# Two encoder layers on one core: the MLP products by one level of Strassen's recursion, with the squared rows kept in DRAM

## The chip, the cores and the metric

The kernel runs on 1 core of one Trainium2 chip. The metric is the device time of one execution in microseconds. Matmuls run on TensorE (PE, with its weight loads as PEld), the other arithmetic on VectorE (DVE), ScalarE (ACT) and GpSimd (POOL); SyncE (SP) issues nearly all DMAs.

## The reference, cut to what matters

Two layers, each with a mixing part (a gated DeltaNet in both directions, a windowed attention, and the sum of both through W_out) and an MLP. x is 1024 rows of 1024 features, D_FF is 4096, everything is float32. The change concerns the last lines of a layer:

```python
mix = (jax.nn.sigmoid(g_ma) * y_a + jax.nn.sigmoid(g_mb) * y_b) @ w_out[l]
x = x + rmsnorm(mix, norm_mix_post[l])

h = rmsnorm(x, norm_mlp_pre[l])                  # 1024 x 1024
u = jnp.square(jax.nn.relu(h @ w_mlp_in[l]))     # 1024 x 4096
x = x + rmsnorm(u @ w_mlp_out[l], norm_mlp_post[l])
```

## The kernel before, in words

A float32 product is made of three fp32r matmuls. Each operand is cut into a high half (a cast on ACT, L149, L165 or L236) and a low half (source minus high half, a subtract on DVE, L150 or L166, or on POOL, L237). `mm3` (L171 to L174) adds high·high, high·low and low·high into one PSUM bank. The moving operand is 128x512, and so is a bank.

A layer goes through stages P1 to P3 (projections, convolution, the two attentions), P4 (output projection, L1060 to L1087) and P5 (MLP, from L1089).

P4 walks the 1024 rows as eight tiles t of 128 rows, four at a time (`hf`), and the output in two column halves `ch`. Per bank there are 24 matmuls (`ps_wo`); DVE copies the bank to `mo` (L1082), ACT squares it for the norm (L1084). After the second half `finish_rows` (L1189) forms the post-norm, adds x, stores the rows to DRAM (`X1d`), forms the MLP's pre-norm, and has `norm_to_T` (L183) transpose the rows on PE (8 transposes of 128x128, L194) and split them into halves: h transposed, `h2T`, in SBUF.

P5 loads W1 and W2 as units of 512 KB (`weight_unit`, L157), splits them, and runs groups of two 128-feature slices: `mlp_in` (L1096) makes u transposed for two slices (per slice and half of the rows 24 matmuls into `ps_m`), with relu and square on ACT (L1113, L1114) and the low half on DVE (L1115, L1116); u stays in SBUF as halves. `mlp_out` (L1119) takes the slices of a group as the contraction and makes for every t and `ch` a partial bank, which DVE adds to an accumulator `acc` in SBUF (L1137). The last group has four slices; there each row tile is finished as soon as its two banks are in (`mlp_finish`, L1148): the norm, the sum with the rows from `X1d`, the store, and in layer 0 the next layer's pre-norm and transposes (`hTn`). The next layer's first matmuls are those of `ps_zA` (128x336, 192 of them), which read `hTn` tile by tile.

The order on an engine is set by a scheduler that works from the code, priorities and buffers; `InOrder` (L140 on) pins an engine's instructions to the order in which they are written. Buffers are pools with a number of copies each: a new tile in a full pool waits for the oldest to be read.

Of the kernel before, what the change touches and what calls it, by code (L numbers as in the profile page):

```python
# [16 lines left out]
P = 128  # L17
# [29 lines left out]
def shape_constants():  # L47
# [28 lines left out]
def trunk(ctx, tc, x, w_in, conv_w, a_log, dt_bias, dn_norm_w, attn_sink, w_up_a, w_up_b, w_out,  # L76
# [12 lines left out]
    # three blocks of 32 KB a partition, handed on from stage to stage  # L89
# [41 lines left out]
    class InOrder:  # L131
        """An engine; what is issued through it stays in the order in which it is written."""
# [24 lines left out]
    def weight_unit(wp, src, kk, n, name):  # L157
# [3 lines left out]
        pw, bw = (wmain, 3) if i % 5 < 3 else (wp, 2)  # L161
# [9 lines left out]
    def mm3(o, lh, ll, rh, rl, first, last, eng=T):  # L171
        eng.matmul(o, lhsT=lh, rhs=rh, start=first, stop=False)  # L172
        eng.matmul(o, lhsT=lh, rhs=rl, start=False, stop=False)  # L173
        eng.matmul(o, lhsT=ll, rhs=rh, start=False, stop=last)  # L174
# [8 lines left out]
    def norm_to_T(pl, xt, wrow, halves, t, tag, tagb, bank=None):  # L183
# [1050 lines left out]
```

## Time and profile before

| what | value |
|---|---|
| median of 3 runs | 3323.45 us (3322.81 to 3325.22) |
| span of the profiled execution | 3319.1 us, 4.3 us under the median |
| PE busy | 3189.2 us, 96% |
| DVE, ACT, POOL busy | 1878.1, 1101.2, 740.4 us |
| first and last `ps_m` matmul, layer 0 | 967.9 to 1672.0 us |
| first and last `ps_m` matmul, layer 1 | 2609.6 to 3310.0 us |
| `ps_m` matmuls | 6144, one third at each line of `mm3` |

The profile is of one execution. A matmul's duration in it (0.39 us) is from its issue to its end; matmuls overlap, so what one costs in a stream is the distance between starts. DVE, ACT and POOL instructions run one after the other on their engine. Waiting time of an engine that nobody waits for costs nothing.

### The profile page before, as it was taken

To read this page: it belongs to the slowest core of one execution; us is meant where nothing else is said; L and a number is where in the kernel's file an instruction comes from. 1 tells how busy PE (TensorE), PEld (TensorE's weight loads), DVE (VectorE), ACT (ScalarE), POOL (GpSimd) and SP (SyncE) were. 2 spreads that over 40 slices of the span, in tenths; PEclk is the share of its full clock that TensorE was granted. 3 is DMA by queue.
4 is the path that set the end of the run, shared out by engine and by line. 5 is a ranking of instruction groups with operands and counts; after the bars stand their busy time and mean duration, and the time that the engine had idled before them with its cause. 6 is when DMAs were issued, how large, how long until landed. Compare 5 with 4: busy or idle time off the path is not lost.

```text
span 3319.1 us, 47199 instructions
## 1 busy us (share of the span) xinstructions
PE 3189.2 (96%) x18576; PEld 2673.1 (81%) x18576; DVE 1878.1 (57%) x3086; ACT 1101.2 (33%) x1976; POOL 740.4 (22%) x712
## 2 busy tenths in 40 slices
PE   8999999997999999999999999998889999999998
PEld 7878767876888888888898887777778888888887
DVE  4687548735573444444556884585356634444445
ACT  3556433322343212211335664333223421112212
POOL 1354454244210000000023544523442000000000
PEclk9999999899999999999999999998989999999999
DMA  3222498596651111111232226966965411111112
GB/s 131 66 65 72 120 274 218 151 237 186 207 171 51 51 51 51 45 51 40 87 110 60 78 67 176 286 173 180 241 184 188 134 45 46 50 51 51 51 51 102
DMA packets 497142, 385.93 MB, mean 116 GB/s; under 512 B 83716, under 2 KB 446980, under 8 KB 496920
## 3 DMA queue, kind: packets, MB, share of 16 engines
q1 hardware_dynamic: 496920, 382.90, 39.8%
q8 instruction: 147, 2.41, 0.3%
q14 instruction: 75, 0.61, 0.1%
HBM read 277.71 MB, written 105.12 MB: 115 GB/s over the span
## 4 chain that ended last, share of the span: by engine, by line
PE 74%; DVE 9%; DMA 6%; POOL 4%; issue 3%; ACT 2%; SPq 2%; POOLq 0%; ACTq 0%; DVEq 0%
PE ps_m L172 14%; PE ps_m L174 14%; PE ps_m L173 14%; PE ps_scO L139 2%; PE ps_wo L173 2%; PE ps_wo L174 2%; PE ps_wo L172 2%; PE ps_gt L172 2%; PE ps_cv L172 2%; PE ps_gt L174 2%; PE ps_cv L173 2%; PE ps_ub L139 2%; PE ps_cv L174 2%; DMA g<-GR 1%; PE ps_gt L173 1%
## 5 line engine op out<-in xcount | busy, mean ns | idle before, releaser
L1137 DVE TENSOR_TENSOR acc<-ps_m,acc 128x512 f32<-128x512 f32 x448 | 306.8, 690 | 459.1 <-PE ps_m L174 458.1
L172 PE MATMUL ps_m<-h2T,w_w 128*128 128x512 f32 x1024 | 399.1, 390 | 1.9 <-DVE h2T L150 1.9
L172 PE MATMUL ps_m<-w_w,u 128*128 128x512 f32 x1024 | 399.1, 390 | 0.0
L173 PE MATMUL ps_m<-h2T,w_w 128*128 128x512 f32 x1024 | 398.9, 390 | 0.0
L173 PE MATMUL ps_m<-w_w,u 128*128 128x512 f32 x1024 | 398.8, 389 | 0.0
L174 PE MATMUL ps_m<-w_w,u 128*128 128x512 f32 x1024 | 398.7, 389 | 0.0
L174 PE MATMUL ps_m<-h2T,w_w 128*128 128x512 f32 x1024 | 398.7, 389 | 0.0
L1113 ACT ACTIVATE ru<-ps_m 128x512 f32<-128x512 f32 x128 | 76.2, 600 | 866.0 <-PE ps_m L174 866.0
L180 POOL TENSOR_TENSOR frs<-fms,mhalf 128x1 f32<-128x1 f32 x16 | 9.7, 606 | 1361.5 <-DVE fms L178 1345.0
L172 PEld LDWEIGHTS ps_m<-h2T,w_w 128*128 128x128 f32 x1024 | 192.3, 188 | 42.1 <-DVE h2T L150 2.4
L174 PEld LDWEIGHTS ps_m<-h2T,w_w 128*128 128x128 f32 x1024 | 192.3, 188 | 39.8
L174 PEld LDWEIGHTS ps_m<-w_w,u 128*128 128x128 f32 x1024 | 192.3, 188 | 39.8
L172 PEld LDWEIGHTS ps_m<-w_w,u 128*128 128x128 f32 x1024 | 192.4, 188 | 39.7
L173 PEld LDWEIGHTS ps_m<-w_w,u 128*128 128x128 f32 x1024 | 192.3, 188 | 39.6
L173 PEld LDWEIGHTS ps_m<-h2T,w_w 128*128 128x128 f32 x1024 | 192.3, 188 | 39.6
L1115 DVE TENSOR_TENSOR ru<-ru 128x512 f32<-128x512 f32 x128 | 88.3, 692 | 236.8 <-ACT ru L1113 236.8
L166 DVE TENSOR_TENSOR w_w<-st_w,w_w 128x1024 fp32r<-128x1024 f32 x128 | 153.7, 1219 | 5.5 <-ACT w_w L165 5.5
L652 DVE TENSOR_TENSOR ct<-ps_kk,g 128x512 f32<-128x512 f32 x128 | 81.7, 683 | 113.3 <-ACT g L636 68.1
L165 ACT CAST w_w<-st_w 128x1024 fp32r<-128x1024 f32 x128 | 130.9, 1043 | 5.7 <-DMA st_w<-in_w_mlp_in_dram 3.9
L468 DVE SCALAR_TENSOR_TENSOR cv<-pad,cw,cv 128x1024 f32<-128x1024 f32 x96 | 131.0, 1365 | 2.5 <-ACT cv L466 1.3
L675 DVE TENSOR_TENSOR tmpx<-ct 128x30 f32<-128x30 f32 (+14 forms) x240 | 114.5, 477 | 30.1 <-ACT ct L670 22.6
L139 PE MATMUL ps_ub<-obT,w_ub 128*128 128x512 f32 x384 | 120.0, 444 | 0.6 <-DVE tb L139 0.6
(343 smaller groups left out, 7041.4 us busy)
## 6 DMA issues: line engine op xcount, KB each, us to landing
LK<-ct SPq DMA_DIRECT2D x64, 512.0 KB, 6.0
st_w<-in_w_mlp_in_dram SPq DMA_DIRECT2D x64, 512.0 KB, 4.3
st_w<-in_w_mlp_out_dram SPq DMA_DIRECT2D x64, 512.0 KB, 3.4
st_g<-in_w_in_dram SPq DMA_DIRECT2D x32, 512.0 KB, 5.3
TG<-tg SPq DMA_DIRECT2D x64, 256.0 KB, 4.5
g<-GR SPq DMA_DIRECT2D x64, 256.0 KB, 6.3
st_wo<-in_w_out_dram SPq DMA_DIRECT2D x32, 512.0 KB, 4.5
TM<-tm SPq DMA_DIRECT2D x16, 512.0 KB, 3.4
```

What stands on the lines that cost most here:

```text
L139: ins = getattr(self.eng, op)(*a, **k)
L165: A.copy(w[:, 0, :kk * n], st[:, :kk * n])
L166: V.tensor_tensor(w[:, 1, :kk * n], st[:, :kk * n], w[:, 0, :kk * n], ALU.subtract)
L172: eng.matmul(o, lhsT=lh, rhs=rh, start=first, stop=False)
L173: eng.matmul(o, lhsT=lh, rhs=rl, start=False, stop=False)
L174: eng.matmul(o, lhsT=ll, rhs=rh, start=False, stop=last)
L468: V.scalar_tensor_tensor(cv, pad[:, j:j + S], wv[:, j:j + 1], cv, ALU.mult, ALU.add)
L652: V.tensor_tensor(las[d][:, :, h], ps.rearrange("p (t a i) -> p t a i", t=2, a=2), ev.unsqueeze(2).to_broadcast([P, 2, 2, P]), ALU.mult)
L675: V.tensor_tensor(tv, Lx[:, k, k + 1:32].unsqueeze(2).to_broadcast([P, n, m]), Xi[:, k, 0:m].unsqueeze(1).to_broadcast([P, n, m]), ALU.mult)
L1113: A.activation(ru[:, 0], ps, AF.Relu)
L1115: V.tensor_tensor(ru[:, 1], ru[:, 0], ru[:, 0], ALU.mult)
L1137: V.tensor_tensor(acc[:, t, cs], ps, acc[:, t, cs], ALU.add)
```

## The change

One level of Strassen's recursion in Winograd's form cuts both operands of a product into 2x2 blocks and makes seven products of blocks in place of eight, with sums of blocks ahead of them and sums of products behind.

P4. ACT copies the bank to `mo` and squares it from there, POOL adds x to the rows (except for the last tile), and `to_forms` takes the place of `norm_to_T`: row tiles 0 to 3 are split as before (`F1`), and tiles 4 to 7 are combined with them into the block sums of h, three of which are first kept in float32 (`raw23`, `raw4`) and split in P5.

W1. A unit is 256 of the 4096 features (16 units, 7 products of 12 matmuls each). The block sums of W1 are made on POOL (`forms_rest`), split, and multiplied in a written order (`To`, an `InOrder` of PE). Products that are added to an earlier one go into the same bank without a new start, and a copy of the bank is taken between (`X`, `uo`). The first two products of the first four units, which need only tiles 0 to 3 of the rows, are issued ahead (`EARLY`). u, squared on DVE, is stored to DRAM (`Ud`), in float32.

W2. The contraction is cut into four groups of 1024 features. Per group four blocks A of u and four blocks B of W2, 1 MB each, are loaded into slots that a table (`PLACES`) names; block sums are made on POOL in halves of 128x1024 (`sums`); each product takes its two operands through `halves` (two casts on ACT and two subtracts on DVE per operand), 48 matmuls into four banks, and DVE adds the banks to that product's accumulator (in group 0 ACT copies them). In the last group POOL adds the accumulators to one another, and `mlp_finish` runs for tiles 0 to 3 at the last product's start and for tiles 4 to 7 behind its banks.

Matmuls per layer of the MLP: 1344 + 1344 after, 1536 + 1536 before.

```diff
+PLACES = (
...
+            def to_forms(t, xn):
+                c0 = (t % 4) * P
+                cs = slice(c0, c0 + P)
+                pvs = []
+                for q in range(2):
+                    ps = ps_ax("ps_nT", "ab"[q])
+                    for k in range(4):
+                        T.transpose(ps[:, k * P:(k + 1) * P], xn[:, (4 * q + k) * P:(4 * q + k + 1) * P], ident)
+                    pvs.append(ps.rearrange("p (k n) -> p k n", n=P))
+                    if t < 4:
+                        split(F1[:, q, 0, :, cs], F1[:, q, 1, :, cs], pvs[q])
+                if t < 4:
+                    return
+                p12, p22 = pvs
+                t1 = p4.tile([P, 4, P], F32, tag="t1", bufs=2, name="t1")
+                t2, t3, t4 = raw23[:, 0, :, cs], raw23[:, 1, :, cs], raw4[:, 0, :, cs]
+                V.tensor_tensor(t1, p12, F1[:, 0, 0, :, cs], ALU.subtract)
+                G.tensor_tensor(t1, t1, F1[:, 0, 1, :, cs], ALU.subtract)
+                V.tensor_tensor(t2, p22, t1, ALU.subtract)
+                A.copy(F2[:, 1, 0, :, cs], t1)
+                G.tensor_tensor(t4, F1[:, 1, 0, :, cs], t2, ALU.subtract)
+                A.copy(t3, p12)
+                V.tensor_tensor(t3, p22, t3, ALU.subtract)
+                G.tensor_tensor(t4, t4, F1[:, 1, 1, :, cs], ALU.add)
+                V.tensor_tensor(F2[:, 1, 1, :, cs], t1, F2[:, 1, 0, :, cs], ALU.subtract)
+                split(F2[:, 0, 0, :, cs], F2[:, 0, 1, :, cs], p22)
...
-                            V.tensor_copy(mo, ps)
-                            jk = p4.tile([P, 512], F32, tag="jk", bufs=2, name="jk")
-                            A.activation(jk, ps, AF.Square, accum_out=sss[tq][:, ch:ch + 1])
+                            A.copy(mo, ps)
+                            A.activation(ps_ax("ps_jk", "c"), mo, AF.Square, accum_out=sss[tq][:, ch:ch + 1])
...
+                def halves(src, n):
+                    w = whl()
+                    hi, lo = (w[:, h, 0:n].rearrange("p (k n) -> p k n", n=src.shape[-1]) for h in range(2))
+                    split(hi, lo, src)
+                    return hi, lo
...
+                    e, s = wsum(), wsum()
+                    G.tensor_tensor(e[:, 0], a21, a22, ALU.add)
+                    G.tensor_tensor(e[:, 1], a11, a21, ALU.subtract)
+                    G.tensor_tensor(s[:, 0], e[:, 0], a11, ALU.subtract)
+                    G.tensor_tensor(s[:, 1], a12, s[:, 0], ALU.subtract)
+                    s13 = halves(e.rearrange("p a k n -> p (a k) n"), 1024)
+                    s24 = halves(s.rearrange("p a k n -> p (a k) n"), 1024)
+                    return s13, s24, halves(a22, 512)
...
+                def product(bank, w, o, b, first):
+                    for k in range(4):
+                        mm3(bank, w[0][:, o + k, :], w[1][:, o + k, :], b[0][:, k, :], b[1][:, k, :],
+                            first and k == 0, k == 3, To, not first)
...
+                early = []
+                def early_second():
+                    wa, a, uo = early[-1]
+                    product(a, wa, 4, b21, False)
+                    A.copy(uo[:, lo5], a)
+                for u in range(EARLY):
+                    wa, a, uo = forms_first(u), ps_mm("ps_a"), u_tile()
+                    product(a, wa, 0, b11, True)
+                    A.copy(uo[:, hi5], a)
+                    if early:
+                        early_second()
+                    early.append((wa, a, uo))
+                early_second()
...
+                    product(c, s13, 0, t1, True)
+                    if was_early:
+                        unit_tail()
+                        A.copy(X[0], uo[:, hi5])
+                    A.copy(X[3], c)
+                    product(a, s24, 0, t2, was_early)
+                    chain(X[1])
+                    product(c, s24, 4, b22, False)
+                    V.tensor_tensor(uo[:, hi5], X[1], c, ALU.add)
+                    squared(uo, uo)
+                    SY.dma_start(Ud[2 * u], uo)
+                    product(a, s13, 4, t3, False)
+                    chain(X[2])
+                    ut = u_tile()
+                    G.tensor_tensor(ut[:, hi5], X[2], X[3], ALU.add)
...
+                def mlp_finish(t):
...
+                    A.activation(flat(jk), a, AF.Square, accum_out=ss)
                     r = rstd_of(p5, ss, 1, 1.0 / D, "f")
-                    V.scalar_tensor_tensor(a, a, r[:, 0:1], wpost2, ALU.mult, ALU.mult)
-                    V.tensor_tensor(xt, xt, a, ALU.add)
+                    V.scalar_tensor_tensor(a, a, r[:, 0:1], flat(wrows["post"]), ALU.mult, ALU.mult)
+                    (G if i == 0 else V).tensor_tensor(flat(xt), flat(xt), a, ALU.add)
...
+                def granules(q, b):
+                    def cut(v, h):
+                        hi, lo = halves(v[:, 2 * h:2 * h + 2], 1024)
+                        return hi, lo
+                    for h in range(2):
+                        yield cut(q, h), cut(b, h)
...
+                n_prod = 0
+                for g in range(NGR):
+                    at = {n: slot[s] for s, n in PLACES[g].items()}
+                    gs = slice(4 * g, 4 * g + 4)
...
+                    def sums(dst, x, y, op):
+                        for h in range(2):
+                            hs = slice(2 * h, 2 * h + 2)
+                            G.tensor_tensor(at[dst][:, hs], at[x][:, hs], at[y][:, hs], op)
+
+                    for m in ("M1", "M2", "M5", "M6", "M3", "M7", "M4"):
+                        if m == "M1":
+                            pair = "A11", "B11"
+                        elif m == "M2":
+                            pair = "A12", "B21"
+                        elif m == "M5":
+                            sums("E", "A21", "A22", ALU.add)
+                            sums("B11", "B12", "B11", ALU.subtract)
+                            pair = "E", "B11"
+                        elif m == "M6":
+                            sums("A21", "A11", "A21", ALU.subtract)
+                            sums("E", "E", "A11", ALU.subtract)
+                            sums("B12", "B22", "B12", ALU.subtract)
+                            sums("B11", "B22", "B11", ALU.subtract)
+                            pair = "E", "B11"
+                        elif m == "M3":
+                            sums("E", "A12", "E", ALU.subtract)
+                            pair = "E", "B22"
+                        elif m == "M7":
+                            pair = "A21", "B12"
+                        else:
+                            sums("B21", "B21", "B11", ALU.subtract)
+                            pair = "A22", "B21"
...
+                            banks = [bank(tq) for tq in range(4)]
+                            order = [(h, k, tq) for h in range(2) for k in range(2) for tq in range(4)]
+                        have = []
+                        for h, k, tq in order:
+                            if h >= len(have):
+                                have.append(next(grs) if not isinstance(grs, list) else grs[h])
+                            if tq >= len(banks):
+                                banks.append(ps_mm("ps_m2", "m"))
+                            uf, wf = have[h]
+                            ts_ = slice(tq * P, tq * P + P)
+                            mm3(banks[tq], uf[0][:, k, ts_], uf[1][:, k, ts_], wf[0][:, k], wf[1][:, k],
+                                (h, k) == (0, 0), (h, k) == (1, 1), To)
+                            if (h, k) != (1, 1):
+                                continue
+                            dst = acc(m, tq)
+                            if final:
+                                for o in {"M2": ("M1",), "M6": ("M1",), "M3": ("M6", "M5"), "M7": ("M6",),
+                                          "M4": ("M7",)}.get(m, ()):
+                                    G.tensor_tensor(dst, dst, acc(o, tq), ALU.add)
+                            if g == 0:
+                                A.copy(dst, banks[tq])
+                            else:
+                                V.tensor_tensor(dst, banks[tq], dst, ALU.add)
+                            if final and m == "M7":
+                                G.tensor_tensor(acc("M5", tq), acc("M5", tq), dst, ALU.add)
+                            if final and m == "M4":
+                                mlp_finish(4 + tq)
...
```

Three places where the order on an engine moves. First, PE between the output projection (`ps_wo`) and the MLP of layer 0. Before, the transposes of a tile (`ps_nT`) stood among the MLP's first matmuls:

```order
L173 MATMUL ps_m_8935<-h2T_8031,w_w_2_8865 128x512
L174 MATMUL ps_m_8935<-h2T_8031,w_w_2_8865 128x512
L194 MATMUL ps_nT<-ident,xn 128x128 x8
L172 MATMUL ps_m_8935<-h2T_8031,w_w_2_8865 128x512
L173 MATMUL ps_m_8935<-h2T_8031,w_w_2_8865 128x512
```

Now 24 early matmuls stand ahead of all transposes of tiles 4 to 7, and the other 72 early ones behind them:

```order
L189 MATMUL ps_wo<-w_wo_8593,mT_7647 128x512
L190 MATMUL ps_wo<-w_wo_8593,mT_7647 128x512
L155 MATMUL ps_a<-F_8025,w_m 128x512 x24
L1093 MATMUL ps_nT<-ident,mo 128x128 x32
L155 MATMUL ps_a<-F_8025,w_m 128x512 x72
```

The 32 transposes moved together, behind the first 24 of the new products. On ACT, at that place, stand the copies of the banks that these 24 fill (`uo<-ps_a`, L1224), the tiles 4 to 7 (`F_8435`) and the split of the block sums `raw` into `F_9004`:

```order
L165 CAST F_8435<-ps_nT 128x4x128
L1107 COPY raw_8026<-ps_nT 128x4x128
L1105 CAST F_8435<-t_8856 128x4x128
L165 CAST F_9004<-raw_8026 128x1024 x2
L165 CAST F_8435<-ps_nT 128x4x128
L165 CAST F_9004<-raw_8026 128x1024 x2
L1224 COPY uo<-ps_a 128x512 x2
L165 CAST w_m<-st_e 128x1024 x2
```

The first copies of `ps_a` moved behind four casts of the finished block sums.

Second, DVE and POOL inside the W2 product. Before, DVE added bank after bank, with the work on the next group's weights and u between, and POOL had from P4 to the last group only the small powers of the norms:

```order
L1115 TENSOR_TENSOR ru<-ru 128x512
L1137 TENSOR_TENSOR acc<-ps_m_11825,acc 128x512
L166 TENSOR_TENSOR w_w_22_12087<-st_w_22_12085,w_w_22_12087 128x1024
L1116 TENSOR_TENSOR u<-ru,u 128x512
L1137 TENSOR_TENSOR acc<-ps_m_11833,acc 128x512
L1137 TENSOR_TENSOR acc<-ps_m_11841,acc 128x512
```

```order
L180 TENSOR_TENSOR prs<-pms,mhalf 128x1 x2
L180 TENSOR_TENSOR nrs<-nms,mhalf 128x1 x2
L180 TENSOR_TENSOR prs<-pms,mhalf 128x1
L180 TENSOR_TENSOR nrs<-nms,mhalf 128x1
L180 TENSOR_TENSOR frs<-fms,mhalf 128x1 x8
```

Now (a stretch of group 1 of layer 0), DVE has per product four subtracts of operand halves and four adds of banks,

```order
L1422 TENSOR_TENSOR accB<-ps_m_11353,accB 128x512
L166 TENSOR_TENSOR w_m<-src_10838,w_m 128x1024 x2
L166 TENSOR_TENSOR w_m<-src_10837,w_m 128x1024
L166 TENSOR_TENSOR w_m<-src_10838,w_m 128x1024
L1422 TENSOR_TENSOR accA<-ps_m_11418,accA 128x512
L1422 TENSOR_TENSOR accA<-ps_m_11419,accA 128x512
L1422 TENSOR_TENSOR accA<-ps_m_11420,accA 128x512
L1422 TENSOR_TENSOR accA<-ps_m_11421,accA 128x512
L166 TENSOR_TENSOR w_m<-src_10837,w_m 128x1024
L166 TENSOR_TENSOR w_m<-src_10838,w_m 128x1024
```

and POOL the block sums one behind the other:

```order
L1364 TENSOR_TENSOR src_10838<-src_10838 128x1024
L1364 TENSOR_TENSOR src_10837<-src_10837 128x1024
L1364 TENSOR_TENSOR src_10838<-src_10838 128x1024
L1364 TENSOR_TENSOR src_10838<-src_10838,src_10837 128x1024
L1364 TENSOR_TENSOR src_10837<-src_10837 128x1024
L1364 TENSOR_TENSOR src_10838<-src_10838 128x1024
```

The subtracts of the next product's operands stand among and behind the adds of this one's banks, and each reads a 128x1024 block that POOL may have made.

Third, PE at the change of layers. Before, the last transposes of layer 0's rows came as two tiles among the `ps_zA` matmuls of layer 1:

```order
L173 MATMUL ps_zA<-w_zA_13509,hTn_0_8846 128x336
L174 MATMUL ps_zA<-w_zA_13509,hTn_0_8846 128x336
L194 MATMUL ps_nT<-ident,xn 128x128 x16
L172 MATMUL ps_zA<-w_zA_13499,hTn_0_8846 128x336
L173 MATMUL ps_zA<-w_zA_13499,hTn_0_8846 128x336
```

Now those of five tiles come together:

```order
L189 MATMUL ps_zA<-w_zA_13203,hTn_0_12824 128x336
L190 MATMUL ps_zA<-w_zA_13203,hTn_0_12824 128x336
L211 MATMUL ps_nT<-ident,accA 128x128 x40
L188 MATMUL ps_zA<-w_zA_13193,hTn_0_12824 128x336
L189 MATMUL ps_zA<-w_zA_13193,hTn_0_12824 128x336
```

120 of the 192 `ps_zA` matmuls stand behind the 40 transposes.

## Rows read from the trace of the kernel before

**Rows 1.** The page's first lines: span, busy time and share of each engine, and the DMA throughput in 40 equal slices of the span.
```profile
span 3319.1 us, 47199 instructions
...
PE 3189.2 (96%) x18576; PEld 2673.1 (81%) x18576; DVE 1878.1 (57%) x3086; ACT 1101.2 (33%) x1976; POOL 740.4 (22%) x712
...
GB/s 131 66 65 72 120 274 218 151 237 186 207 171 51 51 51 51 45 51 40 87 110 60 78 67 176 286 173 180 241 184 188 134 45 46 50 51 51 51 51 102
```

**Rows 2.** Busy time by engine in stretches of the MLP of layer 0 and of layer 1, of P4 of layer 0, and of the ten microseconds at P4's end (length; PE, PEld, DVE, ACT, POOL busy with their instructions; granted clock, DMA share, GB/s).
```profile
968.00:1658.00 690.00, 689.04 (x3061) 571.03 (x3060) 332.22 (x456) 161.10 (x250) 5.62 (x11) 1.00 0.18 57
2609.00:3300.00 691.00, 690.04 (x3057) 571.85 (x3056) 329.22 (x449) 155.30 (x239) 5.25 (x9) 1.00 0.19 58
...
880.00:1000.00 120.00, 118.67 (x555) 98.44 (x554) 81.11 (x109) 50.79 (x93) 10.61 (x17) 1.00 0.52 171
...
960.00:970.00 10.00, 10.00 (x50) 8.38 (x49) 9.07 (x12) 6.67 (x11) 2.50 (x3) 1.00 0.57 195
```

**Rows 3.** Timeline of PE in layer 0's MLP, the first and the last of 50 matmuls in a row (start, duration, both in us).
```profile
992.00 0.39 PE L174 MATMUL ps_m<-h2T,w_w 128*128 128x512 f32 x1
...
1003.10 0.39 PE L172 MATMUL ps_m<-h2T,w_w 128*128 128x512 f32 x1
```

**Rows 4.** Groups of instructions by line and shape, DVE and ACT (busy us, mean ns of one, then the idle time before them).
```profile
L1137 DVE TENSOR_TENSOR acc<-ps_m,acc 128x512 f32<-128x512 f32 x448 | 306.8, 690 | 459.1 <-PE ps_m L174 458.1
L166 DVE TENSOR_TENSOR w_w<-st_w,w_w 128x1024 fp32r<-128x1024 f32 x128 | 153.7, 1219 | 5.5 <-ACT w_w L165 5.5
L150 DVE TENSOR_TENSOR h2T<-ps_nT,h2T 128x512 fp32r<-128x512 f32 x32 | 20.9, 685 | 6.1 <-ACT h2T L149 6.0
L188 DVE SCALAR_TENSOR_TENSOR xn<-xt,nrs,wpre 128x1024 f32<-128x1024 f32 x16 | 20.5, 1282 | 5.7 <-POOL nrs L180 5.2
L1156 DVE TENSOR_TENSOR xt<-xt,acc 128x1024 f32<-128x1024 f32 x16 | 20.3, 1266 | 0.5 <-DMA xt<-X1d 0.2
L165 ACT CAST w_w<-st_w 128x1024 fp32r<-128x1024 f32 x128 | 130.9, 1043 | 5.7 <-DMA st_w<-in_w_mlp_in_dram 3.9 <-DMA st_w<-in_w_mlp_out_dram 1.7
L1135 ACT COPY acc<-ps_m 128x512 f32<-128x512 f32 x32 | 18.7, 586 | 38.9 <-PE ps_m L174 38.9
L186 ACT ACTIVATE xn<-xt 128x1024 f32<-128x1024 f32 x24 | 25.4, 1060 | 29.9 <-DVE xt L1197 25.1 <-DVE xt L1156 4.8
```

**Rows 5.** The same view, POOL.
```profile
L237 POOL TENSOR_TENSOR w_dk<-st_dk,w_dk 128x1024 fp32r<-128x1024 f32 x8 | 19.2, 2405 | 24.7 <-ACT w_dk L236 14.1 <-PE ps_aq L174 10.6
L139 POOL TENSOR_TENSOR ca<-ca,KDt 128x512 f32<-128x512 f32 x16 | 16.5, 1049 | 16.6 <-DMA ca<-TM 16.3
L139 POOL TENSOR_TENSOR St<-St,dec 128x512 f32<-128x512 f32 x28 | 31.2, 1133 | 47.5 <-PE ps_scO L139 47.4
L180 POOL TENSOR_TENSOR frs<-fms,mhalf 128x1 f32<-128x1 f32 x16 | 9.7, 606 | 1361.5 <-DVE fms L178 1345.0 <-DVE nms L178 16.6
```

**Rows 6.** Timeline at two places where a POOL and a DVE instruction, both with two inputs in SBUF, meet: ahead of P4 of layer 0, and at the change of layers (start, duration in us).
```profile
854.91 1.61 POOL L1057 TENSOR_TENSOR ta<-ta,mb 128x512 f32<-128x512 f32 x1 [1.11 <-DVE ta L1056]
855.43 2.17 DVE L166 TENSOR_TENSOR w_wo<-st_wo,w_wo 128x1024 fp32r<-128x1024 f32 x1
...
1671.27 4.95 POOL L237 TENSOR_TENSOR w_zA<-st_zA,w_zA 128x1008 fp32r<-128x1008 f32 x2
1671.72 3.01 DVE L1155 SCALAR_TENSOR_TENSOR acc<-acc,frs,wpost 128x1024 f32<-128x1024 f32 x1
1674.65 0.68 DVE L1137 TENSOR_TENSOR acc<-ps_m,acc 128x512 f32<-128x512 f32 x1
```

**Rows 7.** DMA issues (KB each, median us from issue to landing).
```profile
st_w<-in_w_mlp_in_dram SPq DMA_DIRECT2D x64, 512.0 KB, 4.3
Y<-ct SPq DMA_DIRECT2D x8, 1024.0 KB, 5.9
xt<-X1d SPq DMA_DIRECT2D x16, 512.0 KB, 3.8
```

**Rows 8.** Timeline of PE at the change of layers: the last matmul of layer 0's MLP, the first and the last of the `ps_zA` matmuls, and a tile's transposes between them.
```profile
1671.57 0.39 PE L174 MATMUL ps_m<-w_w,u 128*128 128x512 f32 x1
1671.80 0.31 PE L172 MATMUL ps_zA<-w_zA,hTn 128*128 128x336 f32 x1
1671.95 0.32 PE L173 MATMUL ps_zA<-w_zA,hTn 128*128 128x336 f32 x1
...
1688.34 1.25 PE L194 MATMUL ps_nT<-ident,xn 128*128 128x128 f32 x8 [2.17 <-DVE hTn L150]
...
1712.19 0.32 PE L174 MATMUL ps_zA<-w_zA,hTn 128*128 128x336 f32 x1
```

**Rows 9.** Busy time and granted clock in three stretches there, columns as in rows 2.
```profile
1685.00:1690.00 5.00, 2.42 (x16) 1.58 (x16) 3.77 (x7) 2.61 (x6) 0.82 (x5) 0.97 0.42 144
1690.00:1695.00 5.00, 3.59 (x13) 3.60 (x14) 3.71 (x9) 1.25 (x4) 0.00 (x0) 0.50 0.21 69
1695.00:1700.00 5.00, 5.00 (x30) 5.00 (x29) 1.01 (x2) 0.45 (x1) 0.00 (x0) 0.85 0.11 38
```

**Rows 10.** Timeline of the end of layer 1: the last matmul, and the last tile's norm and sum (the span ends at 3319.1 us).
```profile
3309.57 0.39 PE L174 MATMUL ps_m<-w_w,u 128*128 128x512 f32 x1
3310.34 0.68 DVE L1137 TENSOR_TENSOR acc<-ps_m,acc 128x512 f32<-128x512 f32 x1
...
3312.94 1.28 DVE L1155 SCALAR_TENSOR_TENSOR acc<-acc,frs,wpost 128x1024 f32<-128x1024 f32 x1 [0.73 <-POOL frs L180]
3314.26 1.23 DVE L1156 TENSOR_TENSOR xt<-xt,acc 128x1024 f32<-128x1024 f32 x1
```

More of the change, by code (lines that the diff above doesn't have):

```diff
@@ L169, in weight_unit, with mm3 @@
         return hi, lo
[L171 to L174, printed above, removed]
+    def mm3(o, lh, ll, rh, rl, first, last, eng=T, joins=False):
+        eng.matmul(o, lhsT=lh, rhs=rh, start=first, stop=False, skip_group_check=joins)
+        eng.matmul(o, lhsT=lh, rhs=rl, start=False, stop=False, skip_group_check=joins)
+        eng.matmul(o, lhsT=ll, rhs=rh, start=False, stop=last, skip_group_check=joins)
     def rstd_of(pl, ss, n, inv, tagp, engines=(V, G)):
@@ new lines, in trunk @@
+                early_second()
+                F3 = act_form(2, "F3")
+                b22, t1, t2, t3 = ([f[:, i, h] for h in range(2)] for f in (F2, F3) for i in range(2))
+                t4 = None
+                for src, form in ((raw23[:, 0], t2), (raw23[:, 1], t3), (raw4[:, 0], None)):
+                    if form is None:
+                        F4 = xp.tile([P, 2, 4, 512], F32R, tag="e2", bufs=1, name="F4")
+                        form = t4 = [F4[:, h] for h in range(2)]
+                    for k in range(2):
+                        ks = slice(2 * k, 2 * k + 2)
+                        split(form[0][:, ks], form[1][:, ks], src[:, ks])
@@ new lines, in trunk, with unit_tail, up_unit5, chain @@
+                Xt = xp.tile([P, 1, 4, 512], F32, tag="e1", bufs=1, name="X")
+                X = [Xt[:, 0, i] for i in range(4)]
+                tail = []
+                def unit_tail():
+                    if tail:
+                        tail.pop()()
+                def up_unit5(u):
+                    st = load_unit(u)
+                    was_early = u < EARLY
+                    wa = None if was_early else halves(st[:, :, 0:P], 1024)
+                    s13, s24, w22 = forms_rest(st)
+                    a, c = ps_ax("ps_a", "a"), ps_mm("ps_c", "m")
+                    if was_early:
+                        uo = early[u][2]
+                    else:
+                        b = ps_ax("ps_b", "b")
+                        uo = u_tile()
+                        product(a, wa, 0, b11, True)
+                        unit_tail()
+                        A.copy(X[0], a)
+                        product(b, wa, 4, b21, True)
+                        V.tensor_tensor(uo[:, lo5], X[0], b, ALU.add)
+                    def chain(dst):
+                        if was_early:
+                            V.tensor_tensor(dst, X[0], a, ALU.add)
+                        else:
+                            A.copy(dst, a)
+                    product(c, s13, 0, t1, True)
+                    if was_early:
+                        unit_tail()
+                        A.copy(X[0], uo[:, hi5])
[10 more added lines that the diff above has]
+                    G.tensor_tensor(ut[:, hi5], X[2], X[3], ALU.add)
+                    def last():
+                        product(a, w22, 0, t4, False)
+                        if was_early:
+                            V.tensor_tensor(ut[:, lo5], X[0], a, ALU.add)
+                        else:
+                            A.copy(ut[:, lo5], a)
+                        squared(ut, ut)
+                        SY.dma_start(Ud[2 * u + 1], ut)
+                    tail.append(last)
@@ new lines, in trunk @@
+                for u in range(NU):
+                    up_unit5(u)
+                unit_tail()
+                blks = [p5.tile([P, 1, 4, 512], F32, tag="sw", bufs=2, name="sw") for _ in range(2)]
+                blks += [block(i, [P, 4, 4, 512], F32, f"src{i}") for i in range(2)]
+                slot = {f"s{i}": blks[i][:, 0] for i in range(2)}
+                slot.update({f"{'ab'[i]}{j}": blks[2 + i][:, j] for i in range(2) for j in range(4)})
+                accs = [block(2, [P, 4, 4, 512], F32, "accA"), xp.tile([P, 2, 4, 512], F32, tag="e2", bufs=1, name="accB"),
+                        xp.tile([P, 1, 4, 512], F32, tag="e1", bufs=1, name="accC")]
```

197 lines of the change are left out of this document (108 added, 89 removed).

## The prediction, made before the changed kernel ran

> **What bounds the kernel now.** The page's first lines come first: PE is busy for 96% of the span [rows 1]. A share over the span hides stages, so the table by stretches comes next: in the MLP PE is busy for 689.04 of 690 us and for 690.04 of 691, at the full granted clock, while DVE has work for under half, ACT for under a quarter and POOL for under 1% [rows 2]. So in these 1400 us every matmul removed is worth its distance in the stream, and every wait added is lost in full. What one is worth comes from the timeline: 49 steps from 992.00 to 1003.10, 0.2265 us each, and not the 0.39 us of a duration [rows 3]. Last come the groups of DVE, ACT and POOL, since the change pays in their work [rows 4, 5], and the two places where the MLP begins and ends [rows 2, 8, 10]. At P4's end PE works through, 10.00 of 10 us [rows 2].
>
> **The change part by part.**
>
> 1. Removed matmuls. 1536 + 1536 per layer become 1344 + 1344; two layers save 768 x 0.2265 = 174.0 us. The shapes are the same, 128x512 from halves of the same kind. A sentence of the Trainium skill speaks against this size ("TensorE: Matmul & The Clock Gate", section "Back-to-back issue gap"): it gives about 131 ns per matmul of 512 columns in a sustained stream, by which only 101 us would go and the sum below would end near 3364. The trace disagrees, 50 starts in a row 0.2265 us apart [rows 3], and it decides.
>
> 2. P4 to MLP. PE has 5.4 us of work (24 x 0.2265) behind the last output-projection matmul, then the transposes of tiles 4 to 7, then products that wait for the bank copies of L1224. Those copies stand on ACT behind four casts of the finished block sums, and the casts need the last tile's L1104 and L1108. From the first of the 32 transposes on, DVE has for the four tiles 20 operations of 128x512 at 0.685 us (13.7), three norm scalings at 1.28 and one add at 1.27 [rows 4]: 18.8 us in series. POOL has 12 pieces of 128x512 at 1.05 to 1.13 us [rows 5] in the same chain. Where both engines read two SBUF inputs one stops the other: at 855.43 DVE's subtract took 2.17 us instead of 1.22 because POOL's add ran to 856.52, and at 1671.72 a scaling took 3.01 us between two POOL instructions [rows 6], while an add that reads PSUM took its usual 0.68 there. I add 4 us for it, and 3 us for the last two casts and the copy (2 x 1.04 + 0.59). PE thus waits until about 5.4 + 1 + 19 + 4 + 3 = 32 us behind P4, does 5.4 us of products and 5 of transposes in that time (8 take 1.25 us [rows 8]), and is idle for some 22 us. After an idle stretch the clock was at half: 0.50 in 1690 to 1695, behind five microseconds with PE busy for 2.42, and 0.85 in the next five [rows 9], a loss of about 2.5 + 0.75 us; I take 2 more. So 24 per layer, 48 in all (before: nothing). Bounds: if little of DVE's series overlaps the 5.4 us, 29; if POOL's pieces fall into DVE's PSUM work, 20. Per kernel 40 to 58.
>
> 3. W1. A unit has 84 matmuls, 19.0 us. Against it DVE has 3 conversions at 1.22 and one of half size, two squares at 1.28 and two adds at 0.69, 8.3 us; ACT the same casts at 1.04 and five copies at 0.59, 6.6 us; POOL five sums of 128x512, 5.5; conversions, squares and sums, which read SBUF alone, make 12.4. A unit loads 1 MB and stores 1 MB, 110 GB/s, where the page shows 286 in a slice [rows 1]. All of it is hidden beside PE: 0. If that cover were gone, the shared 12.4 would have to come in series with 6.6 of ACT to reach PE's 19.0.
>
> 4. W2, groups 0 to 2. A group has 7 x 48 matmuls, 76.1 us. It wants 28 conversions at 1.22 (34.2 us of DVE, and 28 casts at 1.04 on ACT), 28 adds of banks at 0.69 (19.3), and 16 block sums of 128x1024 on POOL at 2.4 us (38.4) [rows 4, 5]. Conversions and sums read two SBUF inputs and exclude each other: 72.6 us of PE's 76.1. Adds of banks read PSUM and may run beside a sum; if none did, DVE and POOL together would need 91.9. So a group costs between 0 and 15.8 us. The sums come in clumps, 4 ahead of M5 and 8 ahead of M6 (28.8 us of POOL against the 32.6 us of three products), and every conversion has to be ready for its own half product of 5.4 us, with five buffers. Laid along the order with these durations, PE waits about 4 us in groups 1 and 2 (an estimate). In group 0 the slots come free only when W1's last products have read the block sums, and 1 MB takes 5.9 us to land [rows 7]: 10 us. 18 per layer, 36 in all (0 to 95).
>
> 5. Last group. 28 more POOL sums of 128x512 at 1.05 to 1.13 us add 30 us to what is shared: 102.5 against 76.1. Half of that excess can lie behind PSUM work and behind the last product: 14 per layer, 28 in all (0 to 45).
>
> 6. Change of layers. Before, the `ps_zA` matmuls run for 40.7 us, from 1671.80, right behind the MLP's last, to 1712.5 [rows 8]. Now tiles 0 to 3 are finished beside the last product, 4 to 7 behind it, and tiles 3 to 7 are transposed in one piece with 120 of the 192 `ps_zA` matmuls behind. A tile's chain is a square (1.06), a power (0.6), a scaling (1.28), an add (1.27 on DVE, 2.4 on POOL), a second square and power, a scaling, two subtracts at 0.69 [rows 4, 5]: 5.2 us of DVE, 6.5 us a tile with what it waits for. Eight tiles are 52 us from the start of M4, 41 from its end, since M4 lasts 10.9; with the last tile's transposes and splits (8 us) and 120 steps at 0.15 us (18, from 1671.80 to 1671.95) it is 67. That is 26 more; I take 25, since later work can move forward into the gap (10 to 35).
>
> 7. End. Before 9.1 us lie between the last matmul and the span's end [rows 10]; now four tiles are finished there, with their squares of 1.06 behind each other, instead of one: +5 (0 to 10).
>
> Sum: -174 + 48 + 0 + 36 + 28 + 25 + 5 = -32. The profiled span of 3319.1 becomes 3287.1, and with the 4.3 us by which the median of the runs lies over the span, 3291.
>
> **The rivals.**
>
> R1, the W2 groups are hidden: the sums fill exactly the time of the bank adds, terms 4 and 5 vanish, 3291 - 64 = 3227. For it: 72.6 of 76.1, and ACT and DMA have room. Against it: clumps, five buffers, and 102.5 in the last group.
>
> R2, the shared access decides (slower): DVE's adds of banks stand in order ahead of the next product's subtracts, so that a bank's adds wait for PE's end of a product, the subtracts then meet POOL's next sum, and sums and adds never overlap. Then each of eight groups takes 91.9 us, 126 us instead of terms 4 and 5 (64): 3353. It decides from the point at which a group's series on DVE and POOL is over 76.1; the last group is over it in any case, the other six by how few of 28 adds overlap (under 23 of them). The Trainium skill states it as a rule ("SBUF — State Buffer", section "Who interferes with whom"): the port pair that VectorE and GpSimd share is an exclusive lock, held for a whole instruction. The trace agrees, 2.17 and 3.01 us [rows 6]; whether it binds hangs on the order, which no run here shows yet.
>
> R3, the hand-over is hidden: ACT's copies come early enough, or DVE has finished tiles 4 to 6 while PE is in P4. Then term 2 falls to 8 (one tile's chain less the 5.4 us): 3251. For it: DVE is free for a third of P4, 81.11 of 120 us busy [rows 2]. Against it: the transposes stand behind the 24 matmuls in PE's own order.
>
> That the change does not do what it says would need products that are not shorter by 768 matmuls; the order has 5376, so I give this no chance.
>
> **How the numbers follow.** Forecast 0.47, with its own range 3255 to 3330 from the bounds of terms 2 and 4 to 6 taken halfway; R1 0.13; R3 0.13; R2 0.20; mixtures beyond these, R1 with R3 (3187) or worse than R2, 0.07. The range goes from 3215 (just under R1) to 3356 (just over R2) and leaves about 0.15 out. A measurement of this kernel can tell 0.2%, 6.6 us, from no change: same is 3317 to 3330. Faster has 0.36 of the forecast, R1, R3 and 0.02 of the mixtures, 0.64; same has 0.09 of the forecast and 0.02 of R2, 0.11; slower the rest, 0.25.
>
> **What would show it.** Term 1: W1's units in a steady pace of 19.0 us with PE busy throughout. Term 2: some 20 us of idle PE behind P4 in both layers, ended by L1224 on ACT, and a low clock behind. Terms 4 and 5: idle time before the `ps_m2` matmuls, ended by subtracts of L166, the largest in the last group; POOL sums and L166 longer than 2.4 and 1.22 us where they meet. Term 6: 67 us between the last `ps_m2` and the last `ps_zA` matmul. The prediction is wrong if PE waits in W1, where I have 0, if the DRAM round trip of u shows up as a releaser, or if a group of W2 takes over 90 us.

## The result, and the profile after

3356.31 us median (3355.64 to 3357.74) against 3323.13 us of the kernel before, a ratio of 1.0103 with a 95% interval of 1.0088 to 1.0117: slower, where a gain of 1% was forecast. The span of the profiled execution grew from 3319.1 to 3354.8 us.

The page's first lines [rows 1] after: PE is busy for 105 us less, not the 174 of the removed matmuls, since part of the others ran at half clock and the tail of a matmul ahead of each wait counts as busy too (below); POOL has more than twice its work.

```profile
span 3354.8 us, 46316 instructions
...
PE 3084.0 (92%) x17808; PEld 2557.4 (76%) x17808; DVE 2148.9 (64%) x2884; ACT 1306.5 (39%) x2140; POOL 1561.2 (47%) x1102
```

The table by stretches, of after, cut where PE's work changes [rows 2, 9]: output projection, W1, W2 and change of layers of layer 0, then the same stages of layer 1, the last line being the end. Columns: length; PE, PEld, DVE, ACT, POOL busy; granted clock, DMA share, GB/s.

```profile
861.00:974.00 113.00, 109.92 (x490) 89.87 (x489) 57.93 (x69) 52.61 (x90) 34.60 (x26) 0.98 0.45 155
974.00:1314.00 340.00, 314.66 (x1378) 258.37 (x1377) 182.58 (x176) 119.13 (x166) 136.77 (x97) 0.96 0.39 128
1314.00:1668.00 354.00, 324.37 (x1353) 259.91 (x1352) 298.98 (x201) 130.28 (x146) 251.27 (x97) 0.96 0.27 92
1668.00:1742.00 74.00, 45.04 (x249) 41.42 (x248) 40.37 (x64) 28.80 (x51) 17.95 (x22) 0.77 0.31 104
...
2644.00:2985.00 341.00, 315.64 (x1377) 259.18 (x1376) 183.43 (x176) 119.46 (x166) 139.19 (x98) 0.95 0.38 124
2985.00:3337.00 352.00, 322.14 (x1344) 258.60 (x1344) 295.26 (x202) 132.75 (x151) 256.47 (x99) 0.96 0.27 93
3337.00:3355.00 18.00, 0.41 (x2) 0.00 (x0) 10.22 (x11) 1.15 (x2) 7.13 (x6) 0.59 0.61 223
```

W1 and W2 have 304.4 us of matmuls each (1344 x 0.2265). They take 340 and 354 us in layer 0. In both the granted clock is below 1.00, where the MLP before had 1.00 throughout. In W2 DVE and POOL are busy for 299 and 251 of 354 us. The stages, by first and last matmul:

| stage | before | after | difference |
|---|---|---|---|
| output projection, two layers | 217.1 | 225.2 | +8.1 |
| MLP, two layers | 1404.1 | 1387.6 | -16.5 |
| `ps_zA` after layer 0 | 40.7 | 74.2 | +33.5 |
| end | 9.3 | 17.6 | +8.3 |
| the rest | 1647.9 | 1650.2 | +2.3 |

What PE waited for in W2 of layer 0 (total us, times, longest) is above all the low halves of the operands:

```profile
PE ps_m L155 <- DVE w_m L166: 21.5, 15, 3.2
PE ps_m L155 <- DVE accC L1422: 4.9, 1, 4.9
PE ps_m L155 <- ACT w_m L165: 1.9, 2, 1.2
```

The subtracts that make them took 2.24 us on average, not the 1.22 of [rows 4], and the sums on POOL about 3.1, not the 2.4 of [rows 5]:

```profile
L166 DVE TENSOR_TENSOR w_m<-src,w_m 128x1024 fp32r<-128x1024 f32 x180 | 395.9, 2239 | 66.2 <-ACT w_m L165 65.9
L1364 POOL TENSOR_TENSOR src<-src,src 128x1024 f32<-128x1024 f32 x28 | 88.0, 3154 | 12.5 <-DVE w_m L166 11.6 <-DMA src<-in_w_mlp_out_dram 0.6
```

How that happens is seen in group 1, ahead of M6. Timeline of DVE and POOL, then of PE (start, duration; x4 is four in a row; in brackets the wait and what ended it):

```profile
1423.99 13.41 DVE L166 TENSOR_TENSOR w_m<-src,w_m 128x1024 fp32r<-128x1024 f32 x4
1426.26 3.39 POOL L1364 TENSOR_TENSOR src<-src,src 128x1024 f32<-128x1024 f32 x1
1429.62 6.71 POOL L1364 TENSOR_TENSOR src<-src 128x1024 f32<-128x1024 f32 x2
1436.29 3.38 POOL L1364 TENSOR_TENSOR src<-src,src 128x1024 f32<-128x1024 f32 x1
1437.33 2.47 DVE L1422 TENSOR_TENSOR accA<-ps_m,accA 128x512 f32<-128x512 f32 x4
1439.63 2.34 POOL L1364 TENSOR_TENSOR src<-src 128x1024 f32<-128x1024 f32 x1
1439.72 3.33 DVE L166 TENSOR_TENSOR w_m<-src,w_m 128x1024 fp32r<-128x1024 f32 x1
```

```profile
1434.12 5.74 PE L155 MATMUL ps_m<-w_m 128*128 128x512 f32 x24 [0.76 <-DVE w_m L166]
1443.11 9.07 PE L155 MATMUL ps_m<-w_m 128*128 128x512 f32 x26 [3.24 <-DVE w_m L166]
```

Four subtracts and the sums beside them take turns: 13.41 us for four, 3.35 us each. PE wants four subtracts per product of 10.9 us, one every 2.7 us, with four bank adds between, which read a bank in PSUM and take their usual time beside a sum. So PE runs dry once the buffers are used up. And here it restarts slowly: the 26 matmuls after the wait of 3.24 us took 9.07 us instead of 5.9. The granted clock fell towards 0.50, the lower of its two levels (as in [rows 9]; half clock below):

```profile
1433.00:1440.00 7.00, 6.11 (x26) 4.43 (x24) 7.00 (x7) 2.43 (x3) 7.00 (x3) 1.00 0.01 2
1440.00:1445.00 5.00, 1.89 (x5) 1.51 (x6) 5.00 (x3) 1.77 (x2) 1.97 (x1) 0.74 0.13 25
1445.00:1450.00 5.00, 5.00 (x15) 3.90 (x14) 2.00 (x3) 0.00 (x0) 0.00 (x0) 0.57 1.03 388
```

That price is not fixed. In group 2 of layer 1 the same product waits 3.25 us at the same place, and the matmuls behind it run at full clock (timeline of PE, then the stretch):

```profile
3198.56 11.63 PE L155 MATMUL ps_m<-w_m 128*128 128x512 f32 x50 [3.25 <-DVE w_m L166]
3195.00:3200.00 5.00, 1.75 (x8) 1.22 (x7) 5.00 (x4) 2.09 (x2) 2.43 (x2) 1.00 0.23 55
```

Counted from start to start, W2 loses 30.7 us of layer 0 to waits (PE idle for more than 0.3 us) and 13.1 to 59 matmuls at half clock; in layer 1 32.8 and 11.2 (54 matmuls). Smaller pauses, and in layer 0 two transposed tiles of the next layer, make the other 6.0 and 3.9.

### The profile page after: what moved, and what is told of

It reads as the page before. It is cut to its first block, busy times and chain, and to the rows that moved or that the text cites. A ratio compares the mean times of both kernels' runs of the same rounds, so it can differ in the third digit from the quotient of the medians.

```text
span 3354.8 us, 46316 instructions
## 1 busy us (share of the span) xinstructions
PE 3084.0 (92%) x17808; PEld 2557.4 (76%) x17808; DVE 2148.9 (64%) x2884; ACT 1306.5 (39%) x2140; POOL 1561.2 (47%) x1102
## 4 chain that ended last, share of the span: by engine, by line
PE 56%; DVE 15%; POOL 11%; DMA 7%; issue 6%; ACT 3%; SPq 2%; DVEq 0%; POOLq 0%; ACTq 0%
PE ps_a L155 9%; PE ps_m L155 8%; PE ps_c L155 5%; DVE w_m L166 4%; PE ps_b L155 2%; PE ps_gt L190 2%; PE ps_gt L188 2%; PE ps_gt L189 2%; POOL src L1364 2%; PE ps_cv L188 2%; PE ps_cv L189 2%; PE ps_cv L190 2%; POOL accA L1418 2%; PE ps_scO L155 2%; DVE cv L486 1%
## 5 line engine op out<-in xcount | busy, mean ns | idle before, releaser
L155 PE MATMUL ps_m<-w_m 128*128 128x512 f32 x2688 | 646.4, 402 | 58.4 <-DVE w_m L166 45.5
L155 PEld LDWEIGHTS ps_m<-w_m 128*128 128x128 f32 x2688 | 518.1, 194 | 186.1 <-DVE w_m L166 61.3
L166 DVE TENSOR_TENSOR w_m<-src,w_m 128x1024 fp32r<-128x1024 f32 x180 | 395.9, 2239 | 66.2 <-ACT w_m L165 65.9
L155 PE MATMUL ps_a<-F,w_m 128*128 128x512 f32 x1632 | 387.4, 393 | 19.7 <-ACT uo L1224 18.1
L155 PEld LDWEIGHTS ps_a<-F,w_m 128*128 128x128 f32 x1632 | 309.0, 190 | 87.7 <-ACT uo L1224 19.7
L165 ACT CAST w_m<-src 128x1024 fp32r<-128x1024 f32 x180 | 182.2, 1049 | 278.6 <-PE ps_m L155 169.5
L155 PE MATMUL ps_c<-F,w_m 128*128 128x512 f32 x768 | 186.3, 392 | 4.9 <-ACT X L1276 4.9
L155 PEld LDWEIGHTS ps_c<-F,w_m 128*128 128x128 f32 x768 | 145.1, 189 | 36.0 <-ACT X L1276 5.7
L1364 POOL TENSOR_TENSOR src<-src 128x1024 f32<-128x1024 f32 x44 | 132.3, 3018 | 64.0 <-DMA src<-U 47.7
L695 DVE TENSOR_TENSOR ct<-ct,tmpx 128x30 f32<-128x30 f32 (+14 forms) x240 | 111.4, 464 | 8.1
```

What stands on the lines that cost most here:

```text
L155: ins = getattr(self.eng, op)(*a, **k)
L165: A.copy(dst_hi, src)
L166: V.tensor_tensor(dst_lo, src, dst_hi, ALU.subtract)
L695: V.tensor_tensor(Xi[:, k + 1:32, 0:m], Xi[:, k + 1:32, 0:m], tv, ALU.subtract)
L1364: G.tensor_tensor(at[dst][:, hs], at[x][:, hs], at[y][:, hs], op)
```

## The experiments

The kernels with the sums on DVE, with the three together and with the last additions on DVE ran four times each (spread 6.6 to 10.9 us), the others once, so a few microseconds of a total are not told apart. The groups of W2, in us, are the measure for most of them (76.1 is PE's own work):

| kernel | layer 0 | layer 1 | time |
|---|---|---|---|
| changed | 86.4, 83.6, 85.7, 98.5 | 86.3, 82.2, 83.0, 100.7 | 3356.3 |
| without last adds | 86.4, 82.4, 84.7, 87.1 | 85.0, 82.8, 83.9, 91.2 | 3314.7 |
| without block sums | 76.2, 76.2, 76.2, 87.0 | 76.2, 76.2, 76.2, 88.3 | 3288.3 |
| sums aside | 83.4, 83.6, 84.3, 100.3 | 82.3, 83.4, 83.9, 101.0 | 3351.2 |
| sums on DVE | 76.7, 77.2, 76.4, 90.3 | 76.2, 77.2, 76.4, 95.2 | 3294.6 |
| M7 first | 84.8, 79.4, 78.8, 98.2 | 84.0, 79.0, 79.0, 100.3 | 3330.9 |

**Without the last additions**.

```diff
-                            if final:
+                            if False:
                                 for o in {"M2": ("M1",), "M6": ("M1",), "M3": ("M6", "M5"), "M7": ("M6",),
...
-                            if final and m == "M7":
+                            if False:
```

> Leaves out the 28 POOL additions per layer that join the seven accumulators in the last group (and so part of the computation). If POOL's additions of two SBUF operands and DVE's subtracts taking turns is what stretches the last group (98.5 and 100.7 us), it falls to what groups 1 and 2 take, 82 to 86 us, and the time by 25 to 32 us, to about 3328. If the last group is long because its products wait for loads or for the tiles' finishing work, it stays above 94 and the time within 10 us of 3356.

3314.7 us, 42 less, more than either theory gave. 20.9 us come from the last groups (98.5 to 87.1, 100.7 to 91.2), short of their expected 82 to 86; 8.0 from the change of layers (74.2 to 66.2) and 6.7 from the end, where the additions stood in POOL's order ahead of the tiles' finishing. The other 6 us lie in stages that the edit does not touch. So the additions cost at two places, and the second was not in the theory.

**Without the block sums**. The products that took a sum take a loaded block instead (`pair`).

```diff
-                        for h in range(2):
+                        for h in range(0):
                             hs = slice(2 * h, 2 * h + 2)
                             G.tensor_tensor(at[dst][:, hs], at[x][:, hs], at[y][:, hs], op)
```

> Leaves out the 16 block sums per group of the W2 product (unsummed blocks are multiplied), all loads and the additions of the last group stay. If the sums are the cause, by turns with the subtracts or by POOL's own series, the groups fall to 76 to 78 us (the last to 80 to 88), the subtracts to 1.22 us, no half-clock stretch is left in groups 1 and 2, and the time to 3260 to 3285. If the trip of u through DRAM or the 1 MB loads are the cause, groups 0 to 2 stay at 82 or more and the time above 3330.

3288.3 us, 3 above the expected range. Groups 0 to 2 take 76.2 us each, group 0 too, so the loads of 1 MB and the trip of u through DRAM cost PE nothing by themselves. PE is busy without a break, at the full clock, and beside it DVE's subtracts are 1.34 us on average over the kernel (the last group still has POOL's additions):

```profile
1316.00:1544.00 228.00, 228.00 (x1007) 188.82 (x1007) 135.53 (x139) 99.47 (x112) 0.00 (x0) 1.00 0.39 136
```

**Sums aside**. `aside` is a bf16 tile of 128x1024 that nobody reads; the products take loaded blocks, as in the run ahead.

```diff
-                            G.tensor_tensor(at[dst][:, hs], at[x][:, hs], at[y][:, hs], op)
+                            G.tensor_tensor(aside, at[alt.get(x, x)][:, hs], at[alt.get(y, y)][:, hs], op)
```

> The same 16 POOL sums per group are made from the loaded blocks but written beside, and the products take unsummed blocks, so nobody waits for a sum; only the access to SBUF is still contended. If the turns decide: subtracts that meet a sum take 2.2 to 3.4 us, the groups 82 to 95 us, and the time stays within 3320 to 3365. If POOL's own series decides (a product waits for the last sum of a clump): subtracts at 1.2 us, groups at 76 to 78, and the time within 10 us of the kernel without sums.

3351.2 us, and the groups nearly as long as with sums that are waited for. The subtracts meet the sums as before:

```profile
L166 DVE TENSOR_TENSOR w_m<-src,w_m 128x1024 fp32r<-128x1024 f32 x184 | 436.3, 2417 | 44.3 <-ACT w_m L165 44.3
```

No product waits for a sum here, so POOL's series as such is ruled out: sums that merely run beside the subtracts make nearly the whole loss.

**Sums on DVE**: `V.tensor_tensor` in place of `G.tensor_tensor` in `sums`.

> The 16 block sums per group move from POOL to DVE, which by the durations makes 28 x 1.22 + 16 x 1.22 + 28 x 0.69 = 73 us of DVE work per group against 76.1 of PE, with nothing of POOL beside it in groups 0 to 2. If the turns decide, a sum costs DVE 1.2 us instead of the 2.4 to 3.4 that a subtract loses to POOL: groups 0 to 2 at 77 to 82, the last at 90 to 98, time 3305 to 3335. If DVE's load as such decides, the groups rise above 86 and the time above 3365.

3294.6 us, ratio to before 0.9934 (0.9915 to 0.9954), 10 below the expected range. DVE is busy for 191 of 229 us in groups 0 to 2, alone, and PE hardly waits:

```profile
1316.00:1545.00 229.00, 228.28 (x1004) 187.93 (x1003) 191.04 (x190) 98.90 (x112) 0.00 (x0) 1.00 0.38 134
```

One change of engine makes the changed kernel faster than the one before, by 0.7%.

**M7 ahead of M6 in groups 0 to 2**; its two sums move with it.

```diff
-                    for m in ("M1", "M2", "M5", "M6", "M3", "M7", "M4"):
+                    for m in (("M1", "M2", "M5", "M6", "M3", "M7", "M4") if final else ("M1", "M2", "M5", "M7", "M6", "M3", "M4")):
```

> Groups 0 to 2 only: product M7 goes ahead of M6, so that the eight half-sums that stand ahead of M6 are split into four ahead of M7 and four ahead of M6; all work and all engines stay. If the clump is the cause (subtracts and sums taking turns at 3.4 us a pair, while PE asks for a subtract every 2.7 us), M6's second half falls from 9.0 to 11.9 us to 6 to 8, the groups to 78 to 81, and the time by 15 to 25 us to 3331 to 3341. If the sum of all shared work decides, wherever it stands, the waits move to M7 and the time stays within 8 us of 3356.

3330.9 us, 25 less. Groups 1 and 2 fall to 79 with the same work on the same engines. Group 0, with its sums pressed together by late slots, falls by only 2.

**Weights of the output projection first**: the loads of the first four units stand ahead of `wpost` and `wpre`.

> The first four weight loads of the output projection are issued ahead of the two norm weights. In the changed kernel PE waits 2.8 us for the third weight unit at the start of the projection in both layers and then runs at half clock for six or seven matmuls, 112.7 us from first to last against 108.3 before. If the order of the loads is the cause the stage takes 108.3 to 109 us and the time falls by 6 to 9 us; if the smaller number of weight buffers is, the stage stays at 112 us and the time within 3 us.

The stage takes 107.7 us in both layers, and PE no longer waits 2.8 us for a cast of `w_wo`. The order of the loads was the cause, and not the smaller number of weight buffers. The time, 3344.6, fell by 12; 10 of that are the stage.

**Statistics first**: `mlp_finish` cut in two. Behind the banks of tiles 4 to 7, a tile's finishing follows the statistics of the next tile.

```diff
                             for tq in range(4):
-                                mlp_finish(tq)
+                                finish_stats(tq)
+                            for tq in range(4):
+                                mlp_finish(tq)
```

> The squares and powers of the last norm of tiles 0 to 3 are made together at the start of the last product, and those of tiles 4 to 7 behind each tile's banks, instead of each behind the finishing of the tile ahead; nothing else changes. If the change of layers is long because the tiles' chains run one behind the other (7.2 us a tile), the stretch from the last matmul of the MLP to the end of the first projection falls from 74 us to 50 to 62, the end from 17.4 us to 13 to 17, and the time by 13 to 27 us. If DVE's load (5.2 us a tile) or the half clock holds it, the stretch stays above 66 us.

3338.6 us. The stretch falls from 74.2 to 57.3 us, within the expectation; the end from 17.6 to 16.2, and the last groups grew by 1 to 3 us.

**The three together**: sums on DVE, weights and statistics first.

> Block sums on DVE, weights first and statistics first together. If the three causes are separate their gains add: 3294.6 for the sums on DVE, less 6 to 9 for the weights, less 10 to 24 for the statistics: 3262 to 3280. If the statistics only move DVE's load into the last group, where DVE has 103 us of work with what it shares with POOL, the last group grows and the time stays above 3285.

3272.7 us, 0.9855 (0.9836 to 0.9873). The gains add up, to 22 of the 16 to 33 expected; the last groups take 94.6 us in both layers (90.3 and 95.2 with the sums on DVE alone).

**Plain tiles 4 to 7** (on the changed kernel).

```diff
-                V.tensor_tensor(t1, p12, F1[:, 0, 0, :, cs], ALU.subtract)
-                G.tensor_tensor(t1, t1, F1[:, 0, 1, :, cs], ALU.subtract)
...
+                A.copy(t2, p22)
+                A.copy(t3, p12)
+                A.copy(t4, p12)
+                split(F2[:, 1, 0, :, cs], F2[:, 1, 1, :, cs], p12)
```

> Row tiles 4 to 7 are only split and copied, without the block sums of h (part of the computation is left out): per tile DVE has 2 operations of 128x512 in place of 5 and POOL none in place of 3; PE's order stays, 24 products, 32 transposes, 72 products, and the copies of the first banks stay behind the tiles on ACT. If DVE's series over the four tiles (with POOL's pieces in its way) sets the wait behind P4, PE's idle time there falls from 21.5 us to 8 to 14, W1 from 340 to 325 to 333 us, and the time by 14 to 30 us to 3326 to 3342. If the order of the copies on ACT sets it, or the clock, W1 stays above 336.

3329.8 us. W1 falls from 340.1 to 328.0 and from 341.1 to 328.9; PE's idle time behind P4 in layer 0 from 21.5 to 10.2 us. The series of block sums of h on DVE, with POOL's pieces in it, makes half of that wait; this run does not part the two engines.

**Last additions on DVE too** (on the three together).

> To the kernel with the sums on DVE, the weights first and the statistics first (3272.7 us), the 28 additions of the last group move from POOL to DVE as well: DVE then has 92.3 us in the last group (28 x 1.22 + 16 x 1.22 + 28 x 0.69 + 28 x 0.69) and nothing shared with POOL but the finishing. If the turns with POOL decide the last group (94.6 us), it falls to 90 or less and the time to 3255 to 3268. If DVE's load decides, it stays at 92 to 97 and the time within 6 us of 3272.

3253.1 us, 0.9807 (0.9788 to 0.9825): faster than expected by either. But mostly not where the theory put it: the last groups take 94.3 and 90.5 us (94.6 before), and in layer 0 DVE is busy for 93 of 94:

```profile
1537.00:1631.00 94.00, 81.92 (x345) 66.14 (x344) 93.04 (x114) 38.23 (x48) 19.83 (x13) 0.95 0.10 34
```

Of the gain, 13 us lie behind them, the change of layers at 49.0 (from 58.0) and the end at 13.3 (from 17.5): with the additions on POOL, DVE waited 4.3 us in layer 0 for a power of a norm that stood behind two of them on POOL, and now it does not. In the last group of layer 0 DVE's load is now the bound.

## Why the prediction was wrong

The forecast was 3291, a gain; the time is 3356.3, a loss, just past the range's upper end of 3356. By its own steps:

| step | predicted | measured |
|---|---|---|
| 1 removed matmuls | -174 | -174 |
| 2 hand-over, 3 W1 | 48 | 60 |
| output projection | 0 | 8 |
| 4 and 5, W2 | 64 | 98 |
| 6 change of layers | 25 | 33.5 |
| 7 end | 5 | 8 |
| the rest | 0 | 2 |

Measured values are from the stage lengths: W2 354.2 + 352.2 less 608.8 of matmuls; W1 340.1 + 341.1 less 608.8, less 12 that the MLP before lost itself (1404.1 against 6144 x 0.2265). The steps add up to 68 us over the forecast and the medians to 65, since the median lies 1.5 us over the profiled span here, not 4.3.

The step that failed most is the price of a wait in steps 4 and 5: 64 us forecast, 98 measured. The waits themselves came to 30.7 and 32.8 us per layer, where 18 + 14 = 32 was forecast, with the clump of eight half-sums ahead of M6 as the largest in groups 1 and 2, and 12.8 and 16.2 in the last group for the 14. But a wait was priced at its length. Matmuls at half clock, up to 14 behind a wait, added 13.1 and 11.2 us, and smaller pauses some 10 in all. The trace of before showed such a restart [rows 9], and it was counted at the hand-over alone. Clock and pauses together are half of the miss. The slow matmuls come with the waits, though not behind every one: in groups 0 to 2 the kernels without sums and with sums on DVE have the full clock throughout.

The 10 us for group 0 were near in size (waits of 7.8 and 6.6 us) but not by the path forecast. PE waited there for subtracts and casts of operands, not for loads, and without the sums the group takes 76.2 us. In layer 0 the late load of u did hold back POOL's first sum, after which all 16 half-sums of the group ran back to back beside the subtracts; no run shows what that delay was worth by itself:

```profile
1314.76 5.75 POOL L1364 TENSOR_TENSOR src<-src 128x1024 f32<-128x1024 f32 x2 [2.34 <-DMA src<-U]
```

Step 2 was right in its mechanism and in the size of the idle time: 21.5 us in both layers, 22 forecast, the last wait ended by the copy that was named:

```profile
981.42 1.06 PE L1093 MATMUL ps_nT<-ident,mo 128*128 128x128 f32 x8 [1.02 <-DVE mo L1130]
988.15 1.09 PE L1093 MATMUL ps_nT<-ident,mo 128*128 128x128 f32 x4 [5.66 <-ACT F L165]
993.33 1.09 PE L1093 MATMUL ps_nT<-ident,mo 128*128 128x128 f32 x4 [4.09 <-DVE F L166]
996.67 1.94 PE L1093 MATMUL ps_nT<-ident,mo 128*128 128x128 f32 x8 [2.26 <-DVE mo L1130]
1007.04 7.33 PE L155 MATMUL ps_a<-F,w_m 128*128 128x512 f32 x20 [8.43 <-ACT uo L1224]
```

The 20 products in the last line took 7.33 us where 4.5 is usual. Step 3 failed: it put W1 at nothing, and the prediction named a wait of PE there as a sign of being wrong. PE waits 3.7 and 3.9 us per layer in W1, above all for copies of banks (`uo` and `X`), with slow matmuls behind one of these waits in layer 1. With the slower transposes, some 6 us per layer were missing from steps 2 and 3.

The output projection was costed at nothing, without a reason. The norm weights stand in the load queue ahead of the weight units; a wait of 2.8 us, and 1.4 to 2 us at half clock behind it, followed in each layer, and the run with the weights first shows that this order was the cause.

Step 6 had the chain right (6.5 us a tile forecast) and its length wrong: the last tiles come 7.24 us apart, with PE idle for 5.3 of it, and the transposes of a tile take 1.94 us at half clock, not 1.25.

```profile
1705.79 1.94 PE L211 MATMUL ps_nT<-ident,accA 128*128 128x128 f32 x8 [5.31 <-DVE fms L194]
1713.03 1.94 PE L211 MATMUL ps_nT<-ident,accA 128*128 128x128 f32 x8 [5.30 <-DVE fms L194]
```

Of the rivals R2 had 3353, nearly the measured time, and that is luck. POOL and DVE taking turns, which it shares with the forecast, is what the run with sums aside shows. But its own condition, bank adds that never overlap a sum, was not met: the four adds at 1437.33 ran beside one and took 2.47 us together. It asked 126 us for the eight groups against 98 measured; hand-over, projection and change of layers made up the rest. The Trainium skill's exclusive lock ("SBUF — State Buffer", section "Who interferes with whom") agrees with the 3.35 us a subtract here. R1 came true in groups 0 to 2 once the sums had left POOL, 76.2 to 77.2 us a group, but not in the last group.

## What to carry to other kernels

Where the matrix engine has no slack, price a wait twice: its length, and the matmuls that may run at half clock behind it (here 30.7 us of waits cost 13.1 more, though one wait of 3.25 us cost nothing more). An operation that reads two SBUF operands is not free on POOL when DVE's own of that kind are due: 16 sums of 2.4 us on POOL cost PE 6 to 10 us a group in groups 0 to 2, the same 16 at 1.2 us on DVE cost it about 1 at most. Add work up by clump, between two due times, not by group: 72.6 of 76.1 us looked like a fit, and moving one product forward with the same total gave 25 us back.

## What the runs showed of the hardware that was not expected

POOL and DVE alternate strictly when both have instructions queued that read two SBUF operands, eleven subtracts in a row at the start of W2 in layer 0. A subtract and a sum together take 3.35 to 3.4 us for as long as both queues last, a little less than 1.22 + 2.4. And 16 MB of u written to DRAM and read back per layer, beside 16 MB of W2 in blocks of 1 MB, did not delay PE where no sums were made, as the groups of 76.2 us show.
